# The third head group's q and k projections as seven block products instead of two plain ones

## The chip, the cores and the metric

The kernel runs on one core of a Trainium2 chip. The metric is the device time of one execution in microseconds. A core has a matrix engine (TensorE, PE in the profile, with PEld for its weight loads), VectorE (DVE), ScalarE (ACT), GpSimd (POOL), SyncE (SP), which issues most loads from HBM, and 16 DMA engines. Each engine runs its own list of instructions in order and waits on semaphores for the others.

## The reference

One layer of an encoder on 512 positions of 1024 channels, in float32: a normalisation, one projection to gMLP, q, k, v and gates, two branches (gated MLP, attention), a merge, and an MLP with squared ReLU. The part at stake is the attention's projection: three groups of four heads of 128 channels.

```python
n = rms_norm(h, norm_mix_pre[l])
proj = jnp.einsum('bsd,de->bse', n, w_in[l])          # n: 512 x 1024
z_gmlp, q, k, v, gates = jnp.split(proj, split_points, axis=-1)
...
q = partial_rope(q.reshape(B, S, n_heads, HEAD_DIM))  # 12 heads of 128
k = partial_rope(k.reshape(B, S, n_heads, HEAD_DIM))
for g, (window, dilation) in enumerate(ATTN_PATTERNS):     # (128,1), (512,4), (2048,16)
    o_g, lse_g = dilated_window_attention(q[:, :, sl], k[:, :, sl], v[:, :, sl], dilation, ...)
w_mix = softmax(stack(lses), axis=0); y_b = sum(w_mix * outs)
```

## The kernel before

Float32 accuracy comes from splitting each operand into a high part in the fast format (a copy on ACT, L74 or L79) and a low part (a subtraction on DVE, L75 or L80), and from three matmuls per product: high x high, high x low, low x high. The normalised input is kept transposed, as `nh` and `nl`, channels on the partitions, in eight blocks of 128 channels.

The loop over four heads h is `project_qk(h)`, then `mix(h)`. In a head, the loop over the groups g = 0, 1, 2 makes a q tile and a k tile of 128 x 512. A load brings the raw weights `qkw` for both, 8 blocks x 128 columns of q and of k, in two transfers of 512 KB.

Groups 0 and 1 use `seven_qk`. It takes q and k together as one product in 2 x 2 blocks (halves of the channels, halves of the positions, q and k as the two block rows) and computes it by seven block products instead of eight, in the manner of Strassen and Winograd. The seven weights are three blocks of the raw weights (`ar0`, `ar1`, `a12`) and four sums of blocks (`s`, made by three DVE additions in `seven`, L331, L332 and L336, and split in two pairs). The seven moving operands come from sums of the input made once, `nt`, and from `nh` and `nl` themselves. `product(n, ...)` issues 4 x 3 matmuls of 256 columns (L345). They run in the order 6, 1, 5, 2, 7, 3, 4 into three PSUM banks Y, Z and X; the results are put together by four copies on ACT (two of them snapshots) and five operations on DVE (L407 to L418).

Group 2 uses `feature_tile`: for q and for k one plain product, eight blocks x 3 matmuls of 512 columns (L84 to L86), after a split of the raw weights, 1024 columns each for q and for k. Two ACT copies (L452) take each result out of PSUM: 32 rows to `st` for the rotation, all rows to the tile.

```python
raw = wpool.tile([P] + shape, F32, name=name, tag="raw")            # wload, L64; wpool has bufs=3
return wpool.tile([P, KH, 4, P], F32, name="s", tag="raw")          # wsum
s12 = split2(s[:, :, 2:4])
ar = [split1(raw[:, :, 1], "ar0"), split1(raw[:, :, 2], "ar1")]     # seven
a12 = split1(raw[:, :, 3], "a12")
s34 = split2(s[:, :, 0:2])
```

Raw weights and the sums `s` share one tag with three buffers. The tiles of `split1` (`ar0`, `ar1`, `a12`) have one buffer each, so the next seven's `ar1` can be written only when product 4 of the one before has passed. A buffer is handed on when its last reader is done, and for raw weights of a seven that is as a rule the subtraction of `ar1`.

The order of the instructions on each engine is decided by a scheduler that lays out the whole program in advance; it mixes the products of neighbouring groups and heads, the scores (`psa`, `psb`), the softmax of the same head and `attend` of the head before. After the heads come the v projection of the gMLP (`pv`), the gates (seven products again), the output and the MLP.

Of the kernel before, what the change touches and what calls it, by code (L numbers as in the profile page):

```python
# [12 lines left out]
AF = mybir.ActivationFunctionType  # L13
# [6 lines left out]
KD = D // P  # L20
# [16 lines left out]
def block_kernel(ctx: ExitStack, tc: tile.TileContext, x, norm_mix_pre, w_in, b_gate, ln_v_gain, ln_v_bias,  # L37
                 w_spatial, b_spatial, w_branch_a, w_branch_b, w_out, norm_mix_post, norm_mlp_pre, w_up,
                 w_down, norm_mlp_post, ident_c, rope_c, mask_c, perm_c, out):
    nc = tc.nc  # L40
# [22 lines left out]
    def wload(shape, srcs, name):  # L63
        raw = wpool.tile([P] + shape, F32, name=name, tag="raw")  # L64
        for dst, src in srcs(raw):
            nc.sync.dma_start(dst, src)
        return raw

    def wsplit(raw, pl=None, bufs=None, tag="w", sub=None):
        pl = pl or wpool  # L70
        shape = list(raw.shape)
        hi = pl.tile(shape, F32R, name="hi", tag=tag + "hi", bufs=bufs)
        lo = pl.tile(shape, F32R, name="lo", tag=tag + "lo", bufs=bufs)
        nc.scalar.activation(hi, raw, AF.Copy)  # L74
        (sub or nc.vector).tensor_tensor(lo, raw, hi.bitcast(F32), op=ALU.subtract)  # L75
        return hi, lo
# [5 lines left out]
    def mm3(ps, a, b, start, stop):  # L82
        (ah, al), (bh, bl) = a, b
        nc.tensor.matmul(ps, ah, bh, start=start, stop=False)  # L84
        nc.tensor.matmul(ps, ah, bl, start=False, stop=False)  # L85
        return nc.tensor.matmul(ps, al, bh, start=False, stop=stop)  # L86
# [168 lines left out]
    nhn, nln = nh[:, :, nat], nl[:, :, nat]  # L255
# [32 lines left out]
    def feature_tile(wh, wl, nk, mh, ml, tag="acc"):  # L288
        ps = psA.tile([P, S], F32, name="pf", tag=tag, bufs={"acc": 4, "S": 2, "T": 1, "y": 1}[tag])
        for k in range(nk):  # L290
            mm3(ps, (wh[:, k], wl[:, k]), (mh[:, k], ml[:, k]), k == 0, k == nk - 1)
        return ps
# [9 lines left out]
    def load_v(h):  # L302
        hs = slice(h * HD, (h + 1) * HD)
        v0, v12 = vpool.tile([P, 2, 4, HD], F32R, name="v0s"), vpool.tile([P, 2, 4, HD], F32, name="v12s")
        nc.gpsimd.dma_start(v0.rearrange("p a b c -> p (a b) c"), v0d[:, :, :, hs].rearrange("p a b c -> p (a b) c"))
        for g in range(2):
            nc.gpsimd.dma_start(v12[:, g], v12d[g, :, hs].rearrange("(l r) c -> l r c", r=4))
        heads[h] = v0, v12
# [19 lines left out]
    def seven(raw, sums, split2, split1):  # L328
        raw = raw.rearrange("p (j h) (r c) -> p j (h r) c", h=2, r=2)
        s = sums()  # L330
        nc.vector.tensor_tensor(s[:, :, 0:4:2], raw[:, :, 1:3], raw[:, :, 0:1].to_broadcast([P, KH, 2, P]), op=ALU.add)  # L331
        nc.vector.tensor_tensor(s[:, :, 3], s[:, :, 2], raw[:, :, 1], op=ALU.add)  # L332
        s12 = split2(s[:, :, 2:4])
        ar = [split1(raw[:, :, 1], "ar0"), split1(raw[:, :, 2], "ar1")]
        a12 = split1(raw[:, :, 3], "a12")
        nc.vector.tensor_tensor(s[:, :, 1], s[:, :, 3], raw[:, :, 3], op=ALU.add)  # L336
        s34 = split2(s[:, :, 0:2])
        pick = lambda g, i: [z[:, :, i] for z in g]
        return {1: ar[0], 2: a12, 3: pick(s34, 1), 4: ar[1], 5: pick(s12, 0), 6: pick(s12, 1), 7: pick(s34, 0)}

    def product(n, ps, w, moving, first):
        (wh, wl), (bh, bl) = w[n], moving[n]
        for j in range(KH):
            for i, (a, b) in enumerate(((wh, bh), (wh, bl), (wl, bh))):
                nc.tensor.matmul(ps, a[:, j], b[:, j], start=first and not (j or i), stop=(j == KH - 1 and i == 2), skip_group_check=True)  # L345
# [40 lines left out]
    def seven_qk(raw, g, c2, c1):  # L386

        w = seven(raw.rearrange("p k r c -> p k (r c)"), wsum, wsplit, split1)
        Y, Z, X = [psA.tile([P, 512], F32, name="pg", tag="acc", bufs=4)[:, A] for _ in range(3)]
        if g:  # L390
            view = lambda ps: ps.rearrange("p (l r) -> p r l", r=4)
            half = lambda d, i: d.rearrange("p (r h l) -> p h r l", r=4, h=2)[:, i]
            snap = lambda nm: qkpool.tile([P, 4, 64], F32, name=nm)
        else:
            view = lambda ps: ps
            half = lambda d, i: d[:, (A, B)[i]]
            snap = lambda nm: qkpool.tile([P, 4, 64], F32, name=nm).rearrange("p r l -> p (r l)")
        p1, z5, u2, u3 = snap("p1"), snap("z5"), snap("u2"), snap("u3")
        product(6, Y, w, nmov, True)
        product(1, X, w, nmov, True)  # L400
        taken = nc.scalar.activation(p1, view(X), AF.Copy)
        while behind and not g:
            tc.add_manual_dep(behind.pop().ins, taken.ins.name, mybir.DependencyInfo(mybir.DependencyClass.NoSync, mybir.DependencyReason.DATA), reason="issue_after")
        if pending:
            with tc.issue_after(taken.ins):
                pending.pop()()
        nc.vector.tensor_tensor(u2, view(Y), p1, op=ALU.add)  # L407
        product(5, Z, w, nmov, True)
        nc.scalar.activation(z5, view(Z), AF.Copy)
        product(2, X, w, nmov, False)  # L410
        nc.scalar.activation(half(c1, 0), view(X), AF.Copy)
        product(7, Y, w, nmov, False)
        nc.vector.scalar_tensor_tensor(u3, view(Y), -1.0, p1, op0=ALU.mult, op1=ALU.subtract)
        product(3, Z, w, nmov, False)
        nc.vector.tensor_tensor(half(c1, 1), view(Z), u2, op=ALU.add)
        nc.vector.tensor_tensor(half(c2, 1), u3, z5, op=ALU.subtract)
        product(4, Y, w, nmov, False)
        nc.vector.scalar_tensor_tensor(half(c2, 0), view(Y), -1.0, p1, op0=ALU.mult, op1=ALU.subtract)  # L418
# [10 lines left out]
    def project_qk(h):  # L429
        got, tiles, r0 = {}, [], 0  # L430
        load_v(h) if not h else None
        st = apool.tile([P, S], F32, name="st", bufs=2)
        for g in range(3):
            if g == 2:
                st, tiles, r0 = apool.tile([P, S], F32, name="st", bufs=2), [], 64
                if h:
                    attend(h - 1)
                    load_v(h)
            hd0 = (g * NH + h) * HD
            raw = wload([KD, 2, P], lambda r: [(r[:, :, 0], fcols(w_in, COL_Q + hd0, KD, P)), (r[:, :, 1], fcols(w_in, COL_K + hd0, KD, P))], "qkw")  # L440
            pair = [apool.tile([P, S], F32, name=f"{nm}{g}") for nm in "qk"]
            if g < 2:
                seven_qk(raw, g, *pair)
            for j, d in enumerate(pair):
                i = r0 + 32 * len(tiles)
                if g < 2:
                    nc.scalar.activation(st[i:i + 32], d[0:32], AF.Copy)
                else:
                    ps = feature_tile(*wsplit(raw[:, :, j]), KD, nhn, nln)
                    view = ps.rearrange("p (l r) -> p r l", r=4)  # L450
                    for dst, src in ((st[i:i + 32], view[0:32]), (d, view)):
                        nc.scalar.activation(dst.rearrange("p (r l) -> p r l", r=4), src, AF.Copy)  # L452
                tiles.append(d)
                got["qk"[j], g] = d.rearrange("p (r l) -> p r l", r=4)
            if g:
                back = rotate(st, tiles, r0)
                if g == 1 and h == NH - 2:
                    behind.extend(back[2:])
            if g == 1:
                scores_a(h, split_qk(tiles[:2]))  # L460
        scores_b(h, got)
# [107 lines left out]
    def attend(h):  # L569
        for _ in attend_steps(h):  # L570
            pass
# [119 lines left out]
    for g2 in range(2):  # L691
        raw = wload([KD, 2 * P], lambda r: [(r, fcols(w_in, COL_U + g2 * 2 * P, KD, 2 * P))], "uw")
        for j in range(2):
            g = 2 * g2 + j
            wh, wl = wsplit(raw[:, :, j * P:(j + 1) * P], sub=nc.gpsimd)
            ps = psA.tile([P, S], F32, name="pf", tag="acc" if g else "T", bufs=4 if g else 1)
# [87 lines left out]
    for d in range(GSTD):  # L784
        g2 = gate_rows(d - GSTD)
        raw = gate_raw(d)
        for br in range(2):
            ps = feature_tile(*wsplit(raw[:, :, 1 - br]), KD, nhn, nln)
# [49 lines left out]
    for k0 in range(0, KD, 2):  # L838
        raw = wload([2, D], lambda r: [(r, w_out[k0 * P:(k0 + 2) * P].rearrange("(k p) c -> p k c", p=P))], "wow")
        for j in range(2):  # L840
            wos.append(wsplit(raw[:, j]) if k0 + j < 3 else wsplit(raw[:, j], wopool, tag="wo"))
    raw = wload([KD, 2 * P], lambda r: [(r, fcols(w_up, 0, KD, 2 * P))], "upw")
# [28 lines left out]
    for t in range(4):  # L871
# [18 lines left out]
        r = rstd_of(ss, 1.0 / D)  # L890
# [42 lines left out]
    for i in range(1, NSTD):  # L933
        raw = raw_up(i)
# [64 lines left out]
    def snap(name, bufs=1):  # L999
        return upool.tile([P, 256], F32, name=name, bufs=bufs)  # L1000
# [183 lines left out]
    def rstd(t):  # L1184
        return rstd_of(sums[t], 1.0 / D)
# [26 lines left out]
    for t in range(2):  # L1212
# [5 lines left out]
        r = rstd(2 + t)  # L1218
# [50 lines left out]
```

## Time and profile before

| | |
|---|---|
| time, median of 3 runs | 783.58 us (780.56 to 787.14) |
| profiled execution | 782.17 us, span 780.3 us from first to last instruction |
| mean granted TensorE clock | 0.998 |
| PE busy | 771.0 us in 4821 matmuls |
| DVE busy | 602.5 us in 963 instructions |
| ACT busy | 460.6 us in 747 instructions |
| the twelve loads of qkw | issued by SP between 49.81 and 182.0 us |

A row of a timeline reads: start, duration, engine, line, operation, the tile written and the tiles read, shapes, count; in square brackets the idle time of the engine before it and what ended that. Durations of instructions in a row overlap a little, so the pace of an engine is taken from start to start. In a list of waits the columns are the engine and line that waited, what it waited for, the total in us, the number of times and the longest.

### The profile page before, as it was taken

How to read it: one execution, taken by the hardware profiler on the slowest of the kernel's cores; microseconds unless marked ns; L12 is line 12 of the kernel's file. 1: busy time of each engine (PE TensorE's matmuls, PEld its weight loads, DVE VectorE, ACT ScalarE, POOL GpSimd, SP SyncE). 2: the span in 40 equal slices, each digit the busy share in tenths (PEclk: the TensorE clock that was granted, in tenths of full speed). 3: DMA queues.
4: the chain of work that ended last, by engine and by line, in shares of the span. 5: the costliest groups of instructions: out<-in, count | busy, mean ns of one | idle time of the engine just before them, and what ended most of it. 6: DMA issues, size and time to landing. Idle time of an engine off the chain costs nothing.

```text
span 780.3 us, 12276 instructions
## 1 busy us (share of the span) xinstructions
PE 771.0 (99%) x4821; PEld 693.4 (89%) x4821; DVE 602.5 (77%) x963; ACT 460.6 (59%) x747; POOL 90.8 (12%) x123
## 2 busy tenths in 40 slices
PE   9999999999999999999999999999999999999996
PEld 6888999999988889999998899999999988888885
DVE  6884689888664979778756559988888699978785
ACT  6352468978776545545444557566666756655671
POOL 2310200010104400000000210002121100303010
PEclk9999999999999999999999999999999999999999
DMA  9733744262725433334434522449989998979803
GB/s 313 244 109 111 213 108 109 56 166 81 223 72 144 140 81 99 92 81 131 153 141 135 196 92 71 138 137 246 276 237 240 302 331 309 206 251 213 219 0 109
DMA packets 104749, 128.30 MB, mean 164 GB/s; under 512 B 3265, under 2 KB 75233, under 8 KB 103794
## 3 DMA queue, kind: packets, MB, share of 16 engines
q1 hardware_dynamic: 83920, 83.50, 33.9%
q0 software_dynamic: 20480, 43.61, 22.9%
q8 instruction: 38, 0.62, 0.3%
q10 hardware_dynamic: 290, 0.40, 0.1%
q14 instruction: 21, 0.17, 0.1%
HBM read 117.53 MB, written 26.74 MB: 185 GB/s over the span
## 4 chain that ended last, share of the span: by engine, by line
PE 95%; DMA 2%; ACT 1%; issue 0%; DVE 0%; POOL 0%; POOLq 0%; DVEq 0%; ACTq 0%
PE pacc L993 11%; PE pg L345 10%; PE pd L1083 6%; PE pd L1084 6%; PE pd L1085 6%; PE pgacc L345 6%; PE pf L85 5%; PE pf L84 5%; PE pf L86 5%; PE ptp L993 5%; PE pv L84 4%; PE pv L86 4%; PE pv L85 4%; PE pgS L345 3%; PE pd L84 2%; PE pd L86 2%
## 5 line engine op out<-in xcount | busy, mean ns | idle before, releaser
L1084 PE MATMUL pd<-hl,hhl 128*128 128x512 f32 x224 | 87.1, 389 | 0.0
L1085 PE MATMUL pd<-hl,hhl 128*128 128x512 f32 x224 | 87.0, 389 | 0.0
L1083 PE MATMUL pd<-hl,hhl 128*128 128x512 f32 x224 | 85.3, 390 | 0.0
L993 PE MATMUL pacc<-nt,hl 128*128 128x256 f32 x504 | 67.2, 280 | 0.0
L993 PEld LDWEIGHTS pacc<-nt,hl 128*128 128x128 f32 x504 | 62.6, 188 | 0.2 <-ACT hl L79 0.2
L1083 PEld LDWEIGHTS pd<-hl,hhl 128*128 128x128 f32 x224 | 42.0, 188 | 8.9 <-ACT hl L79 0.2
L1085 PEld LDWEIGHTS pd<-hl,hhl 128*128 128x128 f32 x224 | 42.0, 188 | 8.7
L1084 PEld LDWEIGHTS pd<-hl,hhl 128*128 128x128 f32 x224 | 42.0, 188 | 8.7
L74 ACT ACTIVATE hi<-s 128x1024 fp32r<-128x1024 f32 x30 | 31.7, 1059 | 30.3 <-DVE s L332 8.6
L79 ACT ACTIVATE hl<-dnw 128x1024 fp32r<-128x1024 f32 x32 | 33.2, 1056 | 23.6 <-DMA dnw<-in_w_down_dram 15.4
L80 DVE TENSOR_TENSOR hl<-dnw,hl 128x1024 fp32r<-128x1024 f32 x32 | 38.5, 1221 | 9.0 <-ACT hl L79 8.9
L993 PE MATMUL pacc<-n,hl 128*128 128x256 f32 x336 | 44.9, 280 | 0.5 <-DVE u L1026 0.5
L75 DVE TENSOR_TENSOR lo<-s,hi 128x1024 fp32r<-128x1024 f32 x30 | 36.6, 1223 | 11.0 <-ACT hi L74 10.8
L79 ACT ACTIVATE hl<-s 128x1024 fp32r<-128x1024 f32 x28 | 29.4, 1057 | 26.3 <-DVE s L976 17.9
L84 PE MATMUL pf<-nh,hi 128*128 128x512 f32 x112 | 44.3, 396 | 0.0
L86 PE MATMUL pf<-nh,lo 128*128 128x512 f32 x112 | 44.1, 393 | 0.0
L85 PE MATMUL pf<-nl,hi 128*128 128x512 f32 x112 | 44.0, 393 | 0.0
L993 PEld LDWEIGHTS pacc<-n,hl 128*128 128x128 f32 x336 | 41.8, 188 | 0.7 <-DVE u L1026 0.7
L80 DVE TENSOR_TENSOR hl<-s,hl 128x1024 fp32r<-128x1024 f32 x28 | 34.2, 1221 | 6.9 <-ACT hl L79 6.8
L85 PE MATMUL pv<-lo,nh 128*128 128x512 f32 x96 | 37.6, 391 | 0.0
L86 PE MATMUL pv<-hi,nl 128*128 128x512 f32 x96 | 37.3, 392 | 0.0
L84 PE MATMUL pv<-hi,nh 128*128 128x512 f32 x96 | 36.9, 392 | 0.0
(382 smaller groups left out, 2252.7 us busy)
## 6 DMA issues: line engine op xcount, KB each, us to landing
upw<-in_w_up_dram SPq DMA_DIRECT2D x16, 1024.0 KB, 5.6
qkw<-in_w_in_dram SPq DMA_DIRECT2D x24, 512.0 KB, 5.2
dnw<-in_w_down_dram SPq DMA_DIRECT2D x12, 1024.0 KB, 7.5
gw<-in_w_in_dram SPq DMA_DIRECT2D x16, 512.0 KB, 5.4
t3d<-in_w_down_dram POOLq DMA_DIRECT2D x8, 1024.0 KB, 10.5
t1d<-in_w_down_dram POOLq DMA_DIRECT2D x8, 1024.0 KB, 11.4
slab<-in_w_in_dram SPq DMA_DIRECT2D x6, 1024.0 KB, 10.5
tsum<-in_w_down_dram POOLq DMA_DIRECT2D x6, 1024.0 KB, 9.6
```

The costliest lines, as they stand in the source:

```text
L74: nc.scalar.activation(hi, raw, AF.Copy)
L75: (sub or nc.vector).tensor_tensor(lo, raw, hi.bitcast(F32), op=ALU.subtract)
L79: nc.scalar.activation(hi, src, AF.Copy)
L80: return sub.tensor_tensor(lo, src, hi.bitcast(F32), op=ALU.subtract)
L84: nc.tensor.matmul(ps, ah, bh, start=start, stop=False)
L85: nc.tensor.matmul(ps, ah, bl, start=False, stop=False)
L86: return nc.tensor.matmul(ps, al, bh, start=False, stop=stop)
L345: nc.tensor.matmul(ps, a[:, j], b[:, j], start=first and not (j or i), stop=(j == KH - 1 and i == 2), skip_group_check=True)
L993: ins = nc.tensor.matmul(ps, a[:, j], b[:, j], start=first and not (j or m), stop=(j == KH - 1 and m == 2), skip_group_check=True)
L1083: nc.tensor.matmul(ps, ah, bh, start=start, stop=False, skip_group_check=True)
L1084: nc.tensor.matmul(ps, ah, bl, start=False, stop=False, skip_group_check=True)
L1085: return nc.tensor.matmul(ps, al, bh, start=False, stop=stop, skip_group_check=True)
```

## The change

The third group takes `seven_qk` as well. The branch on g and the two uses of `feature_tile` in `project_qk` go.

```diff
@@ project_qk
             pair = [apool.tile([P, S], F32, name=f"{nm}{g}") for nm in "qk"]
-            if g < 2:
-                seven_qk(raw, g, *pair)
+            seven_qk(raw, g, *pair)
             for j, d in enumerate(pair):
                 i = r0 + 32 * len(tiles)
-                if g < 2:
-                    nc.scalar.activation(st[i:i + 32], d[0:32], AF.Copy)
-                else:
-                    ps = feature_tile(*wsplit(raw[:, :, j]), KD, nhn, nln)
-                    view = ps.rearrange("p (l r) -> p r l", r=4)
-                    for dst, src in ((st[i:i + 32], view[0:32]), (d, view)):
-                        nc.scalar.activation(dst.rearrange("p (r l) -> p r l", r=4), src, AF.Copy)
+                nc.scalar.activation(st[i:i + 32], d[0:32], AF.Copy)
                 tiles.append(d)
                 got["qk"[j], g] = d.rearrange("p (r l) -> p r l", r=4)
```

The scheduler then lays out the whole stage anew. Rows of the order give line, operation, tile written, tiles read and shape; the number behind a name tells one tile of that name from the next. The first place is on DVE, in the first head, where the second seven's last raw block is subtracted. Before, qkw_1040 belongs to the third group and is only split (`lo_1046`, `lo_1077`), and qkw_1180, already there, belongs to the second head:

```order
L75 TENSOR_TENSOR lo_1046<-qkw_1040,hi_1045 128x1024
L418 SCALAR_TENSOR_TENSOR q0_732<-pg_755,p1_758 128x256
L80 TENSOR_TENSOR ar0_1192<-qkw_1180,ar0_1192 128x512
L80 TENSOR_TENSOR ar1_871<-qkw_856,ar1_871 128x512
L407 TENSOR_TENSOR u2_887<-pg_882,p1_885 128x256
L331 TENSOR_TENSOR s_1185<-qkw_1180 128x8x128
L75 TENSOR_TENSOR lo_1077<-qkw_1040,hi_1076 128x1024
```

With the change the same place reads:

```order
L80 TENSOR_TENSOR ar1_871<-qkw_856,ar1_871 128x512
L407 TENSOR_TENSOR u2_887<-pg_882,p1_885 128x256
L75 TENSOR_TENSOR lo_1063<-s_1045,hi_1062 128x1024
L80 TENSOR_TENSOR a12_1058<-qkw_1040,a12_1058 128x512
L413 SCALAR_TENSOR_TENSOR u3_888<-pg_882,p1_885 128x256
L331 TENSOR_TENSOR s_1245<-qkw_1240 128x8x128
```

The third group now has its own sums (s_1045, made earlier), and qkw_1240, the second head's first load, is read five rows after `ar1_871`, the last reader of qkw_856. The second place follows on DVE: the next release, `ar1_1055` (the third group's own), and the next load's first use, `s_1376`. Before there is no such release here; with the change the rows are:

```order
L80 TENSOR_TENSOR ar1_1055<-qkw_1040,ar1_1055 128x512
L423 STREAM_SHUFFLE sw_983<-st_728 128x512
L407 TENSOR_TENSOR u2_1071<-pg_1066,p1_1069 128x256
L75 TENSOR_TENSOR lo_1263<-s_1245,hi_1262 128x1024
L424 TENSOR_TENSOR st_728<-st_728,rope_709 128x512
L425 TENSOR_TENSOR sw_983<-sw_983,rope_709 128x512
L80 TENSOR_TENSOR a12_1258<-qkw_1240,a12_1258 128x512
L426 TENSOR_TENSOR st_728<-st_728,sw_983 128x512
L331 TENSOR_TENSOR s_1376<-qkw_1371 128x8x128
```

Before, the rows there begin with the second head's `ar1`, and the rotation (L423 to L426) and the next low part follow:

```order
L80 TENSOR_TENSOR ar1_1195<-qkw_1180,ar1_1195 128x512
L336 TENSOR_TENSOR s_1316<-s_1316,qkw_1311 128x4x128
L423 STREAM_SHUFFLE sw_983<-st_728 128x512
L424 TENSOR_TENSOR st_728<-st_728,rope_709 128x512
L425 TENSOR_TENSOR sw_983<-sw_983,rope_709 128x512
L75 TENSOR_TENSOR lo_1320<-s_1316,hi_1319 128x1024
L426 TENSOR_TENSOR st_728<-st_728,sw_983 128x512
```

The sums of the load after (s_1316) stood ahead of the rotation; with the change those of the corresponding load (s_1376) stand behind it. The third place is on PE, around product 4 of the first head's second seven (`pg_882<-nt_92,ar1_871`). Before, plain products of the third group (`pf`) lie on both sides of it:

```order
L84 MATMUL pf_1080<-nh_79,hi_1076 128x512
L85 MATMUL pf_1080<-nl_80,hi_1076 128x512
L86 MATMUL pf_1080<-nh_79,lo_1077 128x512
L345 MATMUL pg_882<-nt_92,ar1_871 128x256 x12
L84 MATMUL pf_1080<-nh_79,hi_1076 128x512
```

With the change products 1 and 5 of the third group's seven (pg_1068, pg_1067) lie there:

```order
L345 MATMUL pg_1068<-nh_79,ar0_1052 128x256 x2
L345 MATMUL pg_1068<-nl_80,ar0_1052 128x256
L345 MATMUL pg_1068<-nh_79,ar0_1052 128x256
L345 MATMUL pg_882<-nt_92,ar1_871 128x256 x12
L345 MATMUL pg_1067<-nt_90,hi_1048 128x256 x2
L345 MATMUL pg_1067<-nt_90,lo_1049 128x256
```

Product 6 of the second head's first seven (pg_1266) follows behind pg_1067; before, the other half of pf_1080 stood between product 4 and the second head's first product.

## The prediction

> **What bounds the kernel now.** I read the page's busy times, its slices and its chain first, then what TensorE ever waited for, then the stage in which the changed code runs.
>
> ```profile
> PE 771.0 (99%) x4821; PEld 693.4 (89%) x4821; DVE 602.5 (77%) x963; ACT 460.6 (59%) x747; POOL 90.8 (12%) x123
> PE   9999999999999999999999999999999999999996
> DVE  6884689888664979778756559988888699978785
> PEclk9999999999999999999999999999999999999999
> PE 95%; DMA 2%; ACT 1%; issue 0%; DVE 0%; POOL 0%; POOLq 0%; DVEq 0%; ACTq 0%
> ```
>
> TensorE (PE) is busy in 99% of the span at the full clock and carries 95% of the chain that ended last. Asked for all waits of PE, the trace names five, 3.0 us together, none of them in the attention part:
>
> ```profile
> PE idle L159 <- DVE onesq L59: 1.1, 1, 1.1
> PE pt L186 <- DVE xn L182: 0.7, 1, 0.7
> PE pacc L993 <- DVE u L1026: 0.5, 1, 0.5
> PE pd L84 <- DVE gs L372: 0.5, 1, 0.5
> PE ptp L993 <- ACT hl L79: 0.2, 1, 0.2
> ```
>
> So the kernel now lasts as long as its matmuls take to pass. A change of the matmuls pays in full, as long as VectorE (DVE) and ScalarE (ACT) keep delivering weights in time; any new wait of PE is paid in full too, since nothing behind it has room to give it back. In the slices DVE stands at 6 to 9 tenths where the heads run. A window over three heads (columns: length, then busy us of PE, PEld, DVE, ACT, POOL, the granted clock, DMA share, GB/s) gives the margin:
>
> ```profile
> 101.40:207.50 106.10, 106.10 (x789) 100.92 (x788) 90.90 (x233) 86.02 (x180) 4.84 (x7) 1.00 0.41 111
> ```
>
> DVE works 90.9 of 106.1 us there. It has 15.2 us of room in three heads, some 5 us a head.
>
> **What the change does to TensorE.** For the third group it removes per head two products of 8 x 3 matmuls with 512 columns, 48 in all, and adds seven products of 4 x 3 with 256 columns, 84 in all. The pace of both, start to start:
>
> ```profile
> 178.56 0.40 PE L84 MATMUL pf<-nh,hi 128*128 128x512 f32 x1
> 184.06 0.40 PE L345 MATMUL pg<-nt,hi 128*128 128x256 f32 x2
> 151.97 4.25 PE pg L345 x36
> ```
>
> Between the first two rows 24 matmuls of 512 columns pass in 5.50 us, 0.229 each; the row of the chain has 36 of 256 columns in 4.25 us, 0.118 each. So 48 x 0.229 = 11.0 us become 84 x 0.118 = 9.9 us: 1.08 us saved a head, **4.3 us in four heads**. The count of multiplications falls by an eighth, the time by a tenth. That is all that the change can bring.
>
> **What it does to VectorE.** The paces are start to start in a stretch without waits, and the rows of the qk tile show the shapes:
>
> ```profile
> L331 DVE TENSOR_TENSOR s<-qkw x8: 1215/1222/1226, 55.7 to 179.7; 128x1024 f32<-128x1024 f32 x8
> L75 DVE TENSOR_TENSOR lo<-qkw,hi x8: 1216/1219/1226, 90.4 to 207.8; 128x1024 fp32r<-128x1024 f32 x8
> 111.09 0.68 DVE L425 TENSOR_TENSOR sw<-sw,rope 128x512 f32<-128x512 f32 x1
> 111.69 1.22 DVE L75 TENSOR_TENSOR lo<-s,hi 128x1024 fp32r<-128x1024 f32 x1
> 112.83 0.68 DVE L426 TENSOR_TENSOR st<-st,sw 128x512 f32<-128x512 f32 x1
> 121.42 0.42 DVE L415 TENSOR_TENSOR k<-pg,u 128x256 f32<-128x256 f32 x1
> 121.76 0.42 DVE L418 SCALAR_TENSOR_TENSOR q<-pg,p 128x256 f32<-128x256 f32 x1
> ```
>
> An instruction of 512 columns takes 0.60 us (111.09 to 111.69), one of 1024 takes 1.14 (to 112.83), one of 256 takes 0.34. Removed per head: two splits of 1024, 2.28 us. Added: the three sums of L331, L332, L336 (1.14 + 0.60 + 0.60), two splits of 1024 (2.28), three of 512 (1.80) and five combinations of 256 (1.70), 8.12 us. Net **5.84 us of DVE more per head**, against 5 us of room, and PE now passes a head 1.08 us sooner. ACT gets three splits of 512 and three short copies for four copies out of PSUM, about 1.4 us a head on 86.0 of 106.1: no bound by itself.
>
> **What it does to the weight loads.** Raw weights and the sums `s` share three buffers. A plain third group took one, a seven takes two. In the new order, at the first release shown in the part on the change, qkw_1040, s_1045 and qkw_856 hold all three until `ar1_871` has been subtracted; only then can qkw_1240 be fetched, which `s_1245` reads five DVE rows later. The price of such a handover stands in the trace of before:
>
> ```profile
> 84.72 1.23 DVE L75 TENSOR_TENSOR lo<-s,hi 128x1024 fp32r<-128x1024 f32 x1 [0.81 <-ACT hi L74]
> 85.98 0.99 SPq L66 DMA_DIRECT2D qkw<-in_w_in_dram  x2
> 92.50 0.63 ACT L79 ACTIVATE ar<-qkw 128x512 fp32r<-128x512 f32 x1 [1.52 <-DMA qkw<-in_w_in_dram]
> 49.81 0.37 SPq L66 DMA_DIRECT2D qkw<-in_w_in_dram  x1
> 55.67 0.64 ACT L79 ACTIVATE ar<-qkw 128x512 fp32r<-128x512 f32 x1 [1.27 <-DMA qkw<-in_w_in_dram]
> DMA to landing us min/median/max: 3.8/5.2/7.7
> ```
>
> A subtraction ended at 85.95, the load's two transfers were issued at 85.98, and the first reader, waiting for nothing else, began at 92.50: 6.55 us. The other row gives 5.86 from issue to reader. I take 6.2, between the two. The bounds are 4.3 (the quickest landing, 3.8, with 0.5 for the second issue) and 8.2.
>
> **The sum.** The first such handover starts at a known time. PE's last product of the first seven:
>
> ```profile
> 90.59 1.60 PE L345 MATMUL pg<-nt,ar 128*128 128x256 f32 x12
> 92.03 0.40 PE L345 MATMUL pg<-nt,hi 128*128 128x256 f32 x2
> 79.26 0.40 PE L345 MATMUL pg<-nt,hi 128*128 128x256 f32 x2
> L79 ACT ACTIVATE ar<-qkw x16: 612/630/639, 53.8 to 200.8; 128x512 fp32r<-128x512 f32 x16
> L80 DVE TENSOR_TENSOR ar<-qkw,ar x16: 678/686/693, 54.4 to 201.4; 128x512 fp32r<-128x512 f32 x16
> ```
>
> It ends at 92.03, the order up to it being the same as before; then the `ar1` copy (0.63) and subtraction (0.69) free the buffer at 93.4. From there to `lo_2780`, the first low part of the last head's third seven, I counted DVE's rows in the order: 27 of 1024 columns, 73 of 512, 67 of 256 (22 of them mask additions, taken at the same pace), 6 shuffles at 0.75 and some 57 small ones at 0.10, together 107.5 us by the paces. The same count over the window above gives 87.8 us where the row says 90.9, so I raise it by 1.04: 111.8 us. Into it fall nine handovers. By the order, DVE has 2.5, 4.8, 6.4, 3.6, 5.9, 6.2, 3.7, 5.0 and 5.8 us of work between a release and the first use of the load that it lets go; against 6.2 us the shortfalls are 3.7 + 1.4 + 0 + 2.6 + 0.3 + 0 + 2.5 + 1.2 + 0.4, about 12 us in which DVE stands still. So `lo_2780` is ready at 93.4 + 111.8 + 12 = 217. PE, which begins its first seven at 79.26, has 950 matmuls of 256 columns (112.1 us), 60 of 128 (6.6) and a few tiny ones ahead of the product that needs it: it would be there at 198.3. **It comes 19 us late** by then, spread over waits of up to 5 us, one per product 6 of a seven (1.5, 3.9, 5.0, 8.5, 11.5, 12.6, 17.5, 18.8 us late in running sum). The third heads' plain products, with which PE filled such waits, are gone. Behind the last head TensorE has the v projection, whose DVE work is small, and goes on as before, only later. What stands behind a waiting subtraction on DVE is the softmax of the head before, and that is inside the count.
>
> 19 - 4.3 = +14.7 us, on the profiled execution's 782.17: 796.9, taken as **797 us**. That execution lies 1.4 us under the median of the three runs, 783.58, which reach from 780.56 to 787.14; I sum against it.
>
> By the Trainium skill, "DMA: Bandwidth & Descriptors", section on the anatomy of one DMA, a transfer costs about 2.0 us and its bytes over 436 GB/s; the two halves of a load, 1 MB, would be in after some 4.4 us, and with 4.9 us per handover the estimate would be 5 us of shortfalls and 790 us. The rows above, 5.86 and 6.55, say more, and the page's fit is for GpSimd's queue.
>
> **The rivals.**
> First, the waits are hidden, and only the matmuls count: 782.2 - 4.3 = 778 us, not slower. Its mechanism is DVE's lead at the stage's start: `lo_738`, which PE uses first at 79.26, can be ready long before, and if DVE keeps 19 us of lead through the heads nothing is lost. The point from which it decides is where DVE's room per head exceeds 5.84 us. Against it: the room is 5, and three raw buffers let DVE prepare no more than the next seven. 8%.
> Second, the loads come in time and only DVE's work counts. Then the lateness is 93.4 + 111.8 - 198.3 = 6.9 us, and the time 782.2 + 6.9 - 4.3 = 785. For it: DMA engines are 41% busy in the window and could be quicker than my two rows; waits on a load also let ACT run ahead. 14%.
> Third, PE's clock drops in its new waits. In all forty slices it stands at 9 now, since PE never paused for long. If it fell to half for 3.4 us after each wait of that length, matmuls of 0.118 us would take 0.236, 1.7 us lost each time; my running sum has two to four such waits, so 3 to 7 us more, 800 to 804. The Trainium skill says so ("TensorE: Matmul & The Clock Gate", section on HAM oscillation: no idle gaps of PE above about 3.4 us); no row here shows a drop. 6%.
>
> **How the numbers follow.** My forecast, 787 to 810, has 72%. Its ends are the handover at 4.3 us (shortfalls of about 3, 788) and at 8.2 us (30 of shortfalls would give 814; not each of nine would be the slowest). The range of 784 to 808 takes in the forecast, most of the third rival and the second's 785. A measurement of this kernel tells no more than about 1%, 7.8 us, from no change. Slower by over 1%, above 791.4: the greater part of the forecast and the third rival, 74%. Within 1%: the second rival, the first (778 is within), and the forecast's low end, 24%. Faster by over 1% would need 775.7, more than the matmuls can give: 2%.
>
> **What would show it.** In the changed profile the count of PE instructions rises by 144, and the `pg` groups of L345 grow by 336 as 192 `pf` go. DVE's busy time rises by about 23 us and, in a window over three heads, its share goes from 86% to about 90 or more with the rest of its idle time put down to the qkw DMA. PE gets waits on `pg` released by DVE `lo` L75 or ACT `hi` L74, in sum 15 to 20 us, where none was. SP's issues of qkw wait for DVE `ar` L80. If PE shows no such waits, the first rival is right; if it waits and no DVE or ACT row waits for the qkw DMA, the second. I would be wrong on the size if the loads land in 4 us, or if waits of ACT, which I left out, come on top of DVE's.

## The result and the profile after

The changed kernel takes **799.74 us** (median of 798.99, 799.73, 799.74 and 806.33). The kernel before, run beside it, took 780.56 to 787.14, median 785.29. The ratio of the runs is **1.0246, 95% interval 1.0213 to 1.028**: slower. It was taken without the runs that the chip disturbed, so it is a little larger than that of the two medians, 1.018. The profiled execution of the changed kernel is the one of 806.33 us; where its extra 6.6 us lie is said below.

The page after, in the same parts as before (busy times, two rows of the slices, the chain by engine):

```profile
PE 777.0 (97%) x4965; PEld 702.3 (87%) x4965; DVE 620.2 (77%) x1007; ACT 466.0 (58%) x763; POOL 91.1 (11%) x123
PE   8999989898989999999999999999999899999996
DVE  6884698989956777778765468998878588968785
PE 71%; DVE 14%; DMA 9%; ACT 3%; issue 2%; SPq 0%; POOL 0%; DVEq 0%; POOLq 0%; ACTq 0%
```

TensorE has the 144 matmuls more, it carries 71% of the chain instead of 95%, and where all slices but the last stood at 9 every second one from the sixth to the twelfth is now an 8 (100 to 241 us, the heads and the first products behind them), as are the first and the one at 623 to 643 us. Windows of the changed kernel (length, then busy us of PE, PEld, DVE, ACT, POOL, granted clock, DMA share, GB/s), over three heads and from 60 us to the first product of the output projection:

```profile
101.40:207.50 106.10, 96.30 (x779) 92.47 (x778) 95.84 (x229) 79.26 (x164) 2.97 (x4) 1.00 0.35 95
60.00:430.50 370.50, 355.86 (x2459) 328.80 (x2458) 279.87 (x573) 213.88 (x409) 29.88 (x36) 0.99 0.41 116
```

The second of them in the kernel before:

```profile
60.00:411.38 351.38, 350.86 (x2314) 320.69 (x2312) 261.27 (x529) 208.37 (x394) 29.76 (x36) 1.00 0.44 122
```

PE was busy in all 106.1 us of the three heads and is now busy in 96.3; DVE rose from 90.9 to 95.8. Up to the output projection the changed kernel loses 19.1 us (411.38 to 430.50). PE is idle for 14.6 us of it instead of 0.5, and its busy time is 5.0 us longer although its matmuls should take 4.3 less. In these 9.3 us two drops of the clock hold 3.4 (below); the rest lies in rows that last longer beside a wait, and I haven't divided it further.

What DVE waited for longest (90 to 235 us: us in total, times, longest), and behind it the chain of work that ended last, in order of time, where the first two handovers of the raw buffers lie (start, length, what):

```profile
DVE s L331 <- DMA qkw<-in_w_in_dram: 10.3, 6, 3.2
```

```profile
92.64 0.64 ACT ar L79
...
93.31 0.70 DVE ar L80
...
94.02 0.37 SPq L66
...
94.44 6.45 DMA qkw<-in_w_in_dram
...
101.01 1.23 DVE s L331
...
106.49 0.61 DVE ar L80
...
107.53 5.29 DMA qkw<-in_w_in_dram
...
112.91 1.23 DVE s L331
```

This is the handover as the prediction described it: ar1 is subtracted until 94.01, SP issues the load, and the sums begin at 101.01, 7.0 us later; the second time from 107.10 to 112.91, 5.8 us. No load of qkw was on the chain before. The chain by line, 85 to 232 us (the line is cut by the view itself):

```profile
by line: DMA qkw<-in_w_in_dram 20.0%; DVE lo L75 9.4%; PE pg L345 8.5%; DVE s L331 6.6%; DVE ar L80 6.5%; DMA slab<-in_w_in_dram 5.3%; DVE p L483 4.7%; issue 3.8%; DVE s L336 2.5%; DVE s L332 2.5%; DVE q L418 2.1%; DVE a L80 1.9%; ACT hi L7
```

20% of 147 us, 29 us of the chain, are loads of qkw: a circle of load, sums, splits, release and next load now sets the pace. At its end the v projection inherits it. The chain again, and the granted clock behind it:

```profile
215.97 1.14 DVE lo L75
...
217.79 0.60 DVE ar L80
218.42 7.82 DMA slab<-in_w_in_dram
226.33 1.07 ACT hi L74
227.42 1.22 DVE lo L75
...
230.43 0.34 DVE q L418
230.77 0.08 DVE z L537
230.92 0.50 PE pv L84
```

```profile
228.00:231.00 3.00, 0.89 (x8) 0.72 (x8) 2.62 (x13) 1.04 (x3) 0.56 (x1) 1.00 0.38 137
231.00:234.00 3.00, 3.00 (x9) 2.38 (x10) 2.70 (x8) 2.95 (x7) 0.00 (x0) 0.54 0.88 289
```

lo_2780 is done at 217.1. The first slab of the v projection gets its buffer only from the second ar1 of the last head (done at 218.4) and lands 7.8 us after its issue. Its split then stands on DVE ahead of q (L418), the row that empties a PSUM bank of that second seven (`pv` and `pg` share four banks; the view names the row behind it, z). PE stands idle for 2.1 us of the three before 231, and then its clock is granted at 0.54 for three us. A second drop of the same size follows at 282, behind another pause of 2.1 us, for `vln`: 1.7 us lost each time.

The profiled execution has one more loss that the other three runs, 6.6 to 7.3 us shorter, can't have had in this size. Far behind the heads, where the down projection's weights begin to load (a piece of the chain, PE's longest wait from 405 to 660 us, and the window behind it):

```profile
625.31 13.16 DMA dnw<-in_w_down_dram
```

```profile
PE pacc L986 <- DVE u L1019: 3.7, 1, 3.7
```

```profile
641.52:647.64 6.12, 6.12 (x20) 5.37 (x21) 2.57 (x4) 2.82 (x4) 1.13 (x1) 0.50 0.75 121
```

One load took 13.16 us, PE waited 3.7 us, and behind the wait its clock stood at half for another 6.1 us, 3.1 us lost. The two, less the 0.5 us that PE waited at this place in the kernel before, are 6.3 us, nearly all of the 6.6; the mean clock of this execution, 0.989 where the other three have 0.995 to 0.997, agrees. A wait of 2.6 us at this place, without a drop of the clock, stands also in the profile of e7, whose time is that of the kernel before; so I don't count it to the change.

### The profile page after: what moved, and what is told of

Its sections match the earlier page's. It is cut to its first block, busy times and chain, and to the rows that moved or that the text cites. A ratio compares the mean times of both kernels' runs of the same rounds, so it can differ in the third digit from the quotient of the medians.

```text
span 804.5 us, 12635 instructions
## 1 busy us (share of the span) xinstructions
PE 777.0 (97%) x4965; PEld 702.3 (87%) x4965; DVE 620.2 (77%) x1007; ACT 466.0 (58%) x763; POOL 91.1 (11%) x123
## 4 chain that ended last, share of the span: by engine, by line
PE 71%; DVE 14%; DMA 9%; ACT 3%; issue 2%; SPq 0%; POOL 0%; DVEq 0%; POOLq 0%; ACTq 0%
PE pacc L986 9%; PE pd L1076 6%; PE pd L1077 6%; PE pd L1078 6%; PE pgacc L345 6%; DMA qkw<-in_w_in_dram 4%; PE ptp L986 4%; PE pf L85 3%; PE pf L84 3%; PE pf L86 3%; PE pg L345 3%; PE pv L84 3%; PE pv L85 3%; PE pgS L345 2%; PE pv L86 2%; DVE lo L75 2%
## 5 line engine op out<-in xcount | busy, mean ns | idle before, releaser
L345 PE MATMUL pg<-nt,hi 128*128 128x256 f32 x288 | 54.2, 284 | 4.6 <-DVE q L418 3.1
L74 ACT ACTIVATE hi<-s 128x1024 fp32r<-128x1024 f32 x38 | 40.1, 1054 | 26.7 <-DVE s L332 10.8
L75 DVE TENSOR_TENSOR lo<-s,hi 128x1024 fp32r<-128x1024 f32 x38 | 46.4, 1221 | 8.9 <-ACT hi L74 8.8
L345 PEld LDWEIGHTS pg<-nt,hi 128*128 128x128 f32 x288 | 44.3, 188 | 6.3 <-ACT hi L74 1.9
L80 DVE TENSOR_TENSOR hl<-dnw,hl 128x1024 fp32r<-128x1024 f32 x32 | 38.5, 1220 | 11.1 <-ACT hl L79 11.1
L345 PE MATMUL pg<-nt,lo 128*128 128x256 f32 x144 | 40.5, 282 | 2.0 <-DVE lo L75 2.0
L1066 DVE TENSOR_TENSOR hhl<-hid,hhl 128x1024 fp32r<-128x1024 f32 x24 | 29.3, 1220 | 13.1 <-ACT hhl L1065 13.1
L80 DVE TENSOR_TENSOR hl<-s,hl 128x1024 fp32r<-128x1024 f32 x28 | 34.2, 1221 | 6.2 <-ACT hl L79 5.8
L1065 ACT ACTIVATE hhl<-hid 128x1024 fp32r<-128x1024 f32 x24 | 25.3, 1058 | 22.9 <-PE pd L1078 22.9
```

The lines of the kernel that those rows point to most:

```text
L80: return sub.tensor_tensor(lo, src, hi.bitcast(F32), op=ALU.subtract)
```

## The experiments

A scheduler orders the instructions when the kernel is built, so each edit below also rewrites the order of the heads on every engine. What that can cost without added work is seen in e8. "Ratio" is the time over that of the kernel before, run on the same chip. "Chain" is the share of the qkw loads in the chain that ended last, 85 to 232 us, "DVE waits" the time that DVE stood idle for them there, "at w_out" the first product of the output projection against 411.38 us in the kernel before.

| run | ratio (95%) | chain | DVE waits, us | at w_out, us |
|---|---|---|---|---|
| the change | 1.0246 (1.0213 to 1.028) | 20.0% | 10.3 | +19.1 |
| e1 second ar1 buffer | 1.0128 (1.0075 to 1.0181) | none | none | +7.6 |
| e2 low parts on GpSimd | 1.0249 (1.0203 to 1.0296) | 20.4% | 10.1 | +21.1 |
| e3 both | 1.017 (1.012 to 1.0221) | 8.0% | 1.6 | +12.6 |
| e4 before, 6.0 us of DVE a head | 1.0186 (1.0138 to 1.0234) | 3.8% | 1.8 | +16.3 |
| e5 sevens in two heads | 1.0038 (1.0023 to 1.0053) | none | none | +3.9 |
| e6 before, 3.0 us of DVE a head | 1.0179 (1.0141 to 1.0217) | 11.0% | 2.0 | +11.4 |
| e7 before, third buffer held | 1.0 (0.9984 to 1.0015) | none | 3.1 | +0.1 |
| e8 before, second ar1 buffer | 1.0124 (1.0099 to 1.015) | 12.6% | 6.5 | +8.4 |
| e9 e1 without low parts | 1.0093 (1.0064 to 1.0122) | 3.7% | none | +6.7 |
| e10 e1 without copies back | 1.0068 (1.0037 to 1.0099) | 4.1% | 1.3 | +7.8 |
| e11 copies back on GpSimd | 1.0209 (1.0162 to 1.0255) | none | none | +15.1 |
| e12 the change without low parts | 1.0088 (1.0055 to 1.0121) | 15.2% | 9.2 | +9.8 |

**e1: a second ar1 buffer.** The handover begins late because ar1 has one buffer, which product 4 of the seven before still reads.

```
-        hl = pl.tile([P, 2, KH, P], F32R, name=tag)
+        hl = pl.tile([P, 2, KH, P], F32R, name=tag, bufs=2 if tag == "ar1" and pl is qkpool else 1)
...
-        p1, z5, u2, u3 = snap("p1"), snap("z5"), snap("u2"), snap("u3")
+        p1, z5, u2, u3 = snap("p1"), snap("z5"), snap("u2"), half(c2, 1)
```

> The changed kernel with a second buffer for ar1 (4 KB; to make room, u3 is written straight into its half of c2). By the order of the instructions a load of qkw then has 6.0 to 11.0 us of DVE's work between the release of its buffer and its first use, where it had 2.4 to 5.7. Theory (the handovers of the raw buffers carry the loss): DVE's waits for the qkw DMA, 10 to 13 us over the heads in the changed kernel, fall below 3; the last low part of the last head comes some 15 to 20 us earlier, the v projection's first slab is in by then, and the time is 778 to 788, at or under the kernel before. Rival (only DVE's added work counts): DVE has as much to do as before, so it is as late, 795 to 800, and its waits only change their name. Rival (clock): as the theory, since without pauses the clock doesn't fall; it is not told apart here.

Measured: 792.57 us, ratio 1.0128. The load is gone from the chain (the window over three heads, and the chain by line):

```profile
101.40:207.50 106.10, 98.38 (x815) 96.35 (x814) 99.20 (x240) 81.75 (x168) 2.96 (x4) 1.00 0.37 99
```

```profile
by line: PE pg L345 53.4%; ACT hi L74 5.6%; issue 4.2%; ACT k L427 2.6%; ACT ar L79 2.5%; PE psb L497 2.4%; PE py L616 2.4%; ACT q L427 2.0%; ACT p L552 2.0%; ACT st L445 1.9%; DVE lo L75 1.7%; PE psa L84 1.3%; PE pt L592 1.2%; ACT p L486 1
```

The first slab is in time too: the v projection begins at 223.99 instead of 230.92, and the clock stays at 1.00. It gives back about 9 us (1.0246 to 1.0128), and by the markers 11.5. But it stops halfway: neither theory nor rival named 792. PE still is idle for 7.7 of the 106.1 us with no load on the chain. Another part of what is left lies far behind the heads: at the late load of the down projection PE waits 2.4 us in this profile, and its clock then stands at half for 3.4 us.

**e2 and e3: the low parts of the third group's sums on GpSimd**, alone and with e1's edit.

```
-        w = seven(raw.rearrange("p k r c -> p k (r c)"), wsum, wsplit, split1)
+        w = seven(raw.rearrange("p k r c -> p k (r c)"), wsum, (lambda src: wsplit(src, sub=nc.gpsimd)) if g == 2 else wsplit, split1)
```

> The changed kernel with the two subtractions of 1024 columns (s12, s34) of each third seven on GpSimd: 2.3 us of work a head less for DVE, 9 us in four heads, at 2.4 us each on GpSimd. The handover of the raw buffers stays: by the order the loads now have only 1.3 to 4.9 us of DVE's work to hide in, and the shortfalls grow from about 17 to 23 us. Theory (handovers carry the loss): most of the 9 us is lost again in longer waits for the qkw DMA, 793 to 800, and DVE's wait for qkw rises above the changed kernel's. Rival (DVE's work carries the loss): 9 us earlier, 786 to 791.

> Both edits: a second ar1 buffer and the third seven's two subtractions on GpSimd. Leads of 4.7 to 11.8 us by the order, and 9 us less of DVE's work. Theory: with both gone nothing of DVE is late for TensorE, and the time comes down to what the matmuls save, 4.3 us under the kernel before: ratio 0.993 to 0.998, 777 to 784. If the rival on DVE's work is right this is the one run in which the loss goes, e1 keeping it. If GpSimd's 2.4 us subtractions stand on TensorE's path, 2 to 4 us above e1.

Measured: 802.13 and 795.53 us. e2 leaves the change where it was, with the same waits for the load (10.1 us). e3 is no better than e1, against what I expected. In these two runs a GpSimd subtraction lasts 2.4 us, twice DVE's 1.2, so its result comes later, and e2 and e3 don't show what DVE's relief alone is worth; e9 and e12 ask that without GpSimd.

**e4 and e6: DVE's added work, whole and half**, in the kernel before.

```
+                    for _ in range(0 if j else 10):      # e6: 5
+                        junk = apool.tile([P, S], F32, name="junk")
+                        nc.vector.tensor_tensor(junk.rearrange("p (k c) -> p k c", k=4), raw[:, 0:4, 1], raw[:, 4:8, 1], op=ALU.add)
+                    w = wsplit(raw[:, :, j])
-                    ps = feature_tile(*wsplit(raw[:, :, j]), KD, nhn, nln)
+                    ps = feature_tile(*w, KD, nhn, nln)
```

> The kernel before (plain third group) with ten additions of 512 columns on DVE per head, 6.0 us, ahead of the third group's two splits; their results aren't used. It has the added DVE work of the change and none of its third sums buffer or matmuls. Theory (handovers carry most): DVE's room of 5 us a head takes most of it, 2 to 5 us over the kernel before, 785 to 790. Rival (DVE's work carries all): 12 us or more over it, 796 and up.

> The kernel before with five instead of ten additions of 512 columns on DVE in each head, 3.0 us a head; their results aren't used. Theory (a ceiling with 2.8 us of room a head): nearly all fits, 0 to 4 us over the kernel before. Rival (room of 5 us a head as first counted, and the loss of e4 made only in the tail, where TensorE waits for the last head's softmax and attention): the last head's extra work comes 3 us later instead of 6, so about half of e4's 15 us, 7 to 8.

Measured: 796.72 us in e4 (the median of three executions; a fourth took 2167.06 us and is left out) and 796.53 us in e6, 14 to 15 us over the kernel before with either dose. So room of 5 or of 2.8 us a head, of which both theories spoke, doesn't decide it: the half dose fits into the first, nearly into the second, and costs as much. The trace of e6 shows one way in which it is lost. First DVE's rows, then two of PE's, the last of product 7 and the first of product 4:

```profile
118.67 0.69 DVE L425 TENSOR_TENSOR sw<-sw,rope 64x512 f32<-64x512 f32 x1
119.38 0.69 DVE L451 TENSOR_TENSOR junk<-qkw 128x512 f32<-128x512 f32 x1
119.99 1.22 DVE L75 TENSOR_TENSOR lo<-s,hi 128x1024 fp32r<-128x1024 f32 x1
121.24 0.69 DVE L426 TENSOR_TENSOR st<-st,sw 64x512 f32<-64x512 f32 x1
121.96 0.69 DVE L80 TENSOR_TENSOR q0l<-q,q0h 128x512 fp32r<-128x512 f32 x1
122.57 0.42 DVE L413 SCALAR_TENSOR_TENSOR u<-pg,p 128x256 f32<-128x256 f32 x1
```

```profile
118.28 0.28 PE L345 MATMUL pg<-nt,lo 128*128 128x256 f32 x1
...
123.04 1.69 PE L345 MATMUL pg<-nt,ar 128*128 128x256 f32 x12 [2.48 <-DVE u L413]
```

Product 7 ends at 118.6; from then on u (L413) could be taken out of PSUM, and product 4 may not add to that bank before. DVE takes its rows in order, and five others stand ahead of u: it comes at 122.57, and PE, done with product 3 at 120.56, is idle for 2.48 us. What costs here is a short row behind long ones, not the sum of the rows. Waits for u (L413 and L407) make 6.1 of PE's 8.8 us of waits from 85 to 300 us in e6. They aren't the whole account: the added rows read the third group's raw weights, whose buffer can't be handed on before them, and loads hold 11.0% of e6's chain. So e4 and e6 don't separate DVE's work from the handovers, nor from the new order.

**e5: sevens in two heads only**, on e1's buffers.

```
-            if g < 2:
+            if g < 2 or h in (0, 2):
...
```

> The third group by sevens in heads 0 and 2 alone, plain in heads 1 and 3, with the second ar1 buffer of e1. The matmuls save 2.2 us instead of 4.3, DVE has 5.84 us more in two heads instead of four. Theory (DVE has a ceiling of about 99 busy us in the window of 106, where it stood at 90.9: 2.8 us of room a head, 11 in four): 11.7 us of work against 11 of room, and a plain head after each dear one to give the lateness back, so about what the matmuls save: 778 to 784 where the kernel before has 781 to 782. Rival (each seven costs its part of what e1 lost, whatever stands next to it): half of e1's 11 us, 786 to 788.

Measured: 785.15 us, 1.0038. It lies between the two cases: 3 us above the kernel before, where half of e1's loss would be 5. That a head with plain products lets PE work through such waits would fit, but isn't shown by this. The edit doesn't pay for itself, with 2.2 us of matmuls saved.

**e7 and e8: buffers alone, no work added**, in the kernel before: a tile that only holds the third raw buffer, and e1's edit.

```
+            if g == 2:
+                hold = wpool.tile([P, KH, 4, P], F32, name="hold", tag="raw")
+                nc.vector.tensor_copy(hold[:, 0, 0, 0:2], raw[:, 0, 0, 0:2])
...
+                    if j:
+                        nc.vector.tensor_copy(hold[:, 0, 1, 0:2], hold[:, 0, 0, 0:2])
```

> The kernel before (plain third group) in which a tile of the size of the sums is taken from the raw buffers in each third group and held until its second split, with two copies of 2 columns on DVE: the third buffer of the change without its work. By the order the leads of the qkw loads shrink from 3.1 to 13.6 us to 3.1 to 9.5, the shortfalls against 6.2 grow from 4 to 9 us. Theory (a handover costs only when DVE has no room to catch up): within 2 us of the kernel before. Rival (a handover costs by itself): 4 us or more slower.

> The kernel before with e1's second ar1 buffer and u3 written in place. Leads by the order are no better there (2.8 to 14.1 us, shortfalls of 16 us), since a plain third group has no ar1. Theory: no gain without the sevens, within 3 us of the kernel before, so that what e1 got back belongs to the change's own handovers. Rival (the second buffer helps every kernel): 4 us or more faster, and e1's gain says nothing on the change.

Measured: 782.35 us, no difference, and 791.2 us, 1.24% slower. The waits for the load by engine, first of e7, then of e8:

```profile
ACT ar L79 <- DMA qkw<-in_w_in_dram: 4.4, 2, 2.3
DVE s L331 <- DMA qkw<-in_w_in_dram: 3.1, 2, 1.7
```

```profile
DVE s L331 <- DMA qkw<-in_w_in_dram: 6.5, 5, 2.8
ACT ar L79 <- DMA qkw<-in_w_in_dram: 1.9, 1, 1.9
```

In the kernel before ACT waits 1.5 us for it. Waits of 7.5 us in sum cost nothing in e7, where the load isn't on the chain; 8.4 us in e8, where it holds 12.6% of the chain, go with some 9 us of time. So it seems that a handover can cost by itself, without any added work, which I had excluded for e8 (the order is new as well, so this is argued); and e1's 9 us aren't a gift of the second buffer to every kernel, since here the same edit does the opposite. It also sets the measure for the other rows: with the same work, a second buffer and the order that comes with it moved the time by 9 us.

**e9 and e12: the change without the third group's low parts**, with and without the second ar1 buffer (e12 and e9 differ only in e1's edit).

```
+        def whole(src, tag="whi", pl=wpool):
...
+            nc.scalar.activation(hi, src, AF.Copy)
+            return hi, hi
...
-        w = seven(raw.rearrange("p k r c -> p k (r c)"), wsum, wsplit, split1)
+        w = seven(raw.rearrange("p k r c -> p k (r c)"), wsum, *((whole, lambda src, tag: whole(src, tag, qkpool)) if g == 2 else (wsplit, split1)))
```

> e1 (second ar1 buffer) without the five subtractions of the third group's low parts: the products take the high part twice, so TensorE and ScalarE do the same work, the third group's results are coarser, and DVE has 4.1 us a head less, 16 us in four heads; no GpSimd. Theory (what e1 still loses is DVE's added work): nearly all of it comes back, 777 to 782 where the kernel before has 782. Rival (what e1 still loses is the order in which DVE and ACT serve the products' sums out of PSUM, not the amount of work): TensorE still waits for z, u and q, and half or more of e1's loss stays, 786 to 792.

> The changed kernel, with its single ar1 buffer, without the five low-part subtractions of the third group (high part twice, as in e9): DVE has 4.1 us a head less, the handover of the raw buffers stays. By the order the leads of the loads are 2.3 to 13.9 us, shortfalls of 12.6 us instead of 18.4. Theory (the handover is a loss of its own): DVE still waits 5 us or more for the qkw DMA, the load stays on the chain that ends last, and the time is 5 to 10 us above e9's. Rival (the handover hurts only because DVE is full): as e9 within 3 us.

Measured: 789.36 and 790.18 us, 1.0093 and 1.0088. Taking 16.3 us of work from DVE brings 12 us (the change, 1.0246, to e12), while the load stays on the chain and is waited for almost as long as before (chain by line of e12, DVE's wait in it):

```profile
by line: PE pg L345 34.6%; DMA qkw<-in_w_in_dram 15.2%; issue 4.5%; DVE s L331 2.5%; PE py L622 2.4%; DVE lo L75 2.4%; ACT ar L79 2.4%; DMA v12s<-v12d 2.3%; DVE ar L80 2.2%; ACT p L492 2.2%; ACT hi L391 2.2%; PE psb L503 1.4%; PE pt L598 1.
```

```profile
DVE s L331 <- DMA qkw<-in_w_in_dram: 9.2, 6, 2.3
```

With the second buffer as well nothing more is gained (e9 against e12). So DVE's work and the handovers aren't two losses that add: they look like parts of one circle, of which relieving either gives 9 to 12 us. As e8 moved by 9 us without a change of work, the size of these gains could be the order's as well. And e9, with DVE's work near that of the kernel before and no wait of DVE for the load, is still 7 us slower with 4.3 us of matmuls saved. Its PE waits, 85 to 300 us:

```profile
PE pg L345 <- DVE ca L555: 2.1, 1, 2.1
PE pg L708 <- DVE vln L683: 1.9, 1, 1.9
PE pg L345 <- DVE q L423: 1.2, 1, 1.2
PE pg L345 <- ACT z L414: 0.9, 1, 0.9
PE pg L345 <- ACT hi L74: 0.7, 1, 0.7
```

Single results, each from another line, hold PE up for 0.7 to 2.1 us: nothing of one kind.

**e10 and e11: ScalarE's copies of the rotated rows** (L427) left out of e1, and put on GpSimd.

```
-        return [nc.scalar.activation(d[0:32], ...) for i, d in enumerate(tiles)]
+        return []                                                      # e10
+        return [nc.gpsimd.tensor_copy(d[0:32], ...) for i, d in ...]   # e11
```

> e1 without the copies of the rotated rows back into q and k (L427): eight of 32x512 per head on ScalarE, 0.63 us each, 5 us a head, left out, so the scores use unrotated rows. TensorE and DVE do the same work. Rival (ScalarE's queue, where the copies that wait for DVE's rotation stand ahead of z, p1 and hi): 4 us or more under e1, 780 to 788. Theory (DVE): no more than 3 us under e1's 1.0128, 789 to 793.

> e1 with these eight copies per head on GpSimd instead of left out. If ScalarE's queue is what e1 still loses by, this keeps most of e10's gain as a complete kernel, 781 to 789; if not, within 3 us of e1, 789 to 794. If GpSimd's copies come late for the scores, above e1.

Measured: 788.12 us, 1.0068, whose interval overlaps e1's: a gain of some 5 us isn't proved, and at the output projection there is none (+7.8 us, e1 +7.6). The copies are six a head and not eight (24 in e1's trace), 3.8 us of ScalarE and not 5. In e11, with them on GpSimd, 800.82 us: a copy takes 1.1 to 1.2 us instead of 0.63, and the kernel is slower than e1, 1.0209. No version beat the kernel before.

## Why the prediction was right, and where it was not

The forecast, 797.0 us in 784 to 808 and slower with 0.74, holds: 799.74. By its steps:

- **The matmuls** (-4.3 us): the counts came as said, 144 more, and where nothing waits 36 matmuls of 256 columns still pass in 4.26 us (on e1's chain). The saving itself was measured by no run alone.
- **The handover** (6.2 us, nine of them): right in place, releaser and size: 7.0 and 5.8 us in the first two, 5.7 to 7.0 in the six for which DVE waited, and SP's issue behind ar1 (L80) in the first seven; the last two loads were issued behind a low part of the sums (L75, at 189.0 and 203.0). The Trainium skill's fit of a transfer ("DMA: Bandwidth & Descriptors", section on the anatomy of one DMA), 4.9 us by the prediction's estimate, is shorter than each of these six; it is for GpSimd's queue, and these loads come from SP's. DVE's shortfalls, predicted as 12 us, are 10.3 us of waits in the trace. lo_2780, due at 217, was done at 217.1.
- **PE's lateness** (19 us): by the markers 19.1 + 4.3 = 23.4 us up to the output projection, by the ratio 1.0246 x 782.2 - 782.2 + 4.3 = 23.5. The sum was 4.5 us short; the time is only 2.7 us off because the execution that I summed against, 782.17, is 1.6 us above the time that the ratio goes by (799.74 / 1.0246 = 780.6). Two steps were mis-sized, in opposite directions. PE's due time of 198.3 was too early: the trace has 92 matmuls of 128 columns ahead of that product, not 60 (those of `psb`, and of `py` with `ptb`, stand twice), some 3.5 us more. The product begins at 217.69, so that PE was some 15 us late there and not 19: idle for 9.8 us (the line below), the rest in rows that last longer beside a wait. And TensorE behind the last head did not go "on as before, only later": the first slab waits for the same buffers, PE pauses for 2.1, 0.6 and 2.1 us, and the clock falls twice, 3.4 us in all, together another 8 us. These 8 us too little and 3.5 too much make up the 4.5; that one hid part of the other is luck.

```profile
79.26:217.69 138.43, 128.63 (x1051) 124.72 (x1050) 120.36 (x277) 99.17 (x202) 7.89 (x11) 1.00 0.37 101
```

- **The division of the 19 us**, 6.9 of DVE's work and 12 of handovers, failed although the total nearly stood. It said that with the loads in time 785 us would be left (the second rival). e1 is that case and has 1.0128, 792 us on the same base. The premise was that DVE has 5 us of room a head which work can fill; e4 and e6, which lose as much with 3 us as with 6, speak against it: an idle share of a queue that is served in order isn't room for a row that stands ahead of a waited-for one. And the two terms seem to overlap: in e12 the larger part of the loss is gone with the loads waited for almost as long.
- **Which waits PE would show**: I named lo (L75) and hi (L74), 15 to 20 us in sum. The sum is 14.6 us up to the output projection. lo is there, but PE waits more for results of the sevens that DVE must take out of PSUM, 4.5 us for q and u, or 6.6 with the wait of `pv` put down to z (85 to 300 us, after):

```profile
PE pg L345 <- DVE q L418: 3.1, 3, 1.6
...
PE pv L84 <- DVE z L537: 2.1, 1, 2.1
PE pg L345 <- DVE lo L75: 2.0, 3, 0.8
PE pg L345 <- ACT z L409: 1.6, 2, 1.3
PE pg L345 <- DVE u L413: 1.4, 2, 0.9
```

- **DVE's busy time** rose by 17.7 us, not 23; rows that follow each other at once overlap and count once, so a fuller queue shows less than the sum of its rows. This is argued, not measured.
- **The rivals.** The first, 778, didn't occur: PE had no lead that lasted. The second's price, 785, isn't what e1 shows. The third occurred beside the forecast: the drop to half costs the 1.7 us that it named, twice up to the output projection, and 3.1 us behind the late load. The rule of the Trainium skill on which it stood ("TensorE: Matmul & The Clock Gate", section on HAM oscillation: idle gaps above about 3.4 us) doesn't give the condition seen here: the first two drops came behind pauses of 2.1 us, only the last behind one of over 3.4.

What stays open: of the 23.5 us, 9 to 14 go when the circle of DVE's work and loads is relieved (e1, e12, e9, e10). The other 10 to 14 stay in these four; in e9's trace they show as short waits of PE for single results, with the plain products gone that lay between them (e5 has half of these and loses 3 us). How much of either part is the scheduler's order, and how much no order could avoid, wasn't separated: no run held the order fixed, and e8 moved by 9 us without a change of work.

## What to carry to other kernels

An engine that is idle for 14% of a stage need not have 14% of room when it serves another engine in order: ask which short row the bound engine waits for and what stands ahead of it. When buffers go round in a circle (load, compute, release), price the whole circle and not only its parts: here the gains of relieving two of them did not add. And where a scheduler orders the instructions, run a control that brings a new order and no new work, before believing a difference of a per cent.

## What the runs showed of the hardware

TensorE's granted clock fell to half in the changed kernel twice behind pauses of 2.1 us, for 3.4 us, and once behind one of 3.7 us, for 6.8 us. In e1 it fell behind 2.4 us, for 3.4 us; in e8 behind pauses of 1.5 and 0.4 us close together, for 3.4 us and with the same loss of 1.7 us; in e3 behind 2.1 and 1.1 us, for 6.8 us, 3.4 us lost. It did not fall behind 2.5 us in e6, 2.6 us in e7 or 2.1 us in e9, so the length of a pause alone doesn't decide it. A load of 1 MB in two transfers took 5.2 to 6.5 us from issue to landing on the chain, and one of the same size took 13.2 us while the DMA engines were 98% busy (625 to 638.5 us).
